# Cross attention of a streaming encoder on Trainium2: keys turned by VectorE's block transpose instead of TensorE

## The chip, the cores and the metric

The kernel runs on one core of a Trainium2 chip (trn2). A core has TensorE (matrix multiplications, with a separate path that loads the stationary operand), VectorE, ScalarE, GpSimd, and SyncE, which here only issues DMA transfers. In the profile they are PE (PEld for the weight loads), DVE, ACT, POOL and SP. The metric is the device time of one execution in microseconds; lower is better.

## What is computed

The reference is one inference step of a two-layer encoder. Each layer has a mixer, a cross attention to a memory, and a SwiGLU block. The change touches the cross attention, which runs twice (once per layer):

```python
def cross_attn(h, mk, mv, w_q, w_o):
    b, t, _ = h.shape
    q = (h @ w_q).reshape(b, t, X_HEADS, X_HEAD_DIM)
    s = jnp.einsum('bqhd,bkhd->bhqk', q, mk).astype(jnp.float32) * X_SCALE
    p = jax.nn.softmax(s, axis=-1).astype(mv.dtype)
    o = jnp.einsum('bhqk,bkhd->bqhd', p, mv).reshape(b, t, X_WIDTH)
    return o @ w_o
```

There are 4 heads of 256 dimensions and 256 memory tokens. One prompt stream of 512 rows attends to keys and values that the kernel computed itself earlier in the step (`memory_kv`; the kernel keeps them in DRAM as `kvd`). Eight running streams of 16 rows each attend to their own cached keys and values, `cache_mem_k` and `cache_mem_v`, of shape (2, 8, 256, 4, 256). All is float32.

## The kernel before

The 640 rows (512 prompt, 128 sample) stay in SBUF in `X`. Products of activations and weights are made in three passes: both operands are split into a rounded high part and the rest (`split_unit`, lines 142 to 153, for weights; `evac_split`, lines 220 to 226, for activations), and high x high, high x low, low x high are added up in PSUM (`PASSES`, `gemm`, lines 191 to 208). A weight unit holds 1024 floats per partition; there are two buffers for the raw unit, three each for the high and low parts.

Scores need the queries and the keys with the head's dimensions on the partitions. The memory's keys lie with the tokens on the partitions after a plain load, so they have to be turned.

`cross_phase` (line 811) is run for layer 0 and layer 1. Its pieces, each a list of small steps:

- `q_list(h)` (line 822) loads the q weights of head h as two units, one per 128 columns (`dt`), each over all eight k-blocks of 128 rows, and makes q with the weights as the stationary operand: 2 halves of 320 columns x 2 `dt` x 24 matmuls (8 k-blocks, 3 passes). Before, its list has 14 steps.
- `load_key(n)` (line 917) asks for the n-th cached key block (one stream, one head, 256 tokens x 256 dimensions, 256 KB) with one DMA into one of four `kr` buffers. `AHEAD = 3`: the step that uses block n asks for block n+3.
- `sample_list(pr, bq)` (line 925) treats two heads and four streams: eight `keys` steps, four loads of values, then `scores`, `trans`, `values`, `turn`. Its `keys` step (line 929) turns a block with four TensorE transposes of 128x128 into a PSUM bank (line 938) and copies it to `KT`, every other one by VectorE (line 942) and by ScalarE (line 944).
- `prompt_list(h)` (line 859) treats one head of the prompt: `load` (two DMAs, line 866), `keys` (four transposes, line 873, then the split of keys and values), and twice `scores`, `trans`, `values`.
- `out_list(h)` (line 999) multiplies the head's output by `w_o` and adds it to `X` (`add_x`, line 316).

`merge` (line 210) deals the steps of several lists into one order by their relative place in their list. After the q of heads 0 and 1, four merges follow, and then the rest of the output projection:

```python
merge(sample_list(0, 0), prompt_list(0), q_list(2))
merge(sample_list(0, 1), prompt_list(1), q_list(3))
merge(sample_list(1, 0), prompt_list(2), out_steps(0))
merge(sample_list(1, 1), prompt_list(3), out_steps(1))
```

This order is a priority: the framework plans the order of each engine's instructions from it and may let a later instruction that is ready pass one that waits. Each engine then works its own instructions strictly in that planned order, and SyncE issues all DMA transfers in one queue. A buffer's next use waits for the last reader of its former content.

The same block transpose on VectorE is already used for the cached keys of layer 0's mixer (line 678), whose blocks are asked for in four DMAs of 32 partitions each (line 670), and for the cached latents of layer 1's mixer (line 1550, loads at line 1545).

Of the kernel before, what the change touches and what calls it, by code (L numbers as in the profile page):

```python
# [18 lines left out]
P = 128  # L19
D = 1024  # L20
KD = D // P
# [71 lines left out]
def fox_mla_kernel(ctx: ExitStack, tc: tile.TileContext, I, O):  # L93
# [717 lines left out]
    def cross_phase(l, nx, rest):  # L811
        w_q, w_o = I["w_x_q"][l], I["w_x_o"][l]
        mk = I["cache_mem_k"][l].rearrange("b (m p) h d -> p (b m) (h d)", p=P)
        mv = I["cache_mem_v"][l].rearrange("b (m p) h d -> p (b m) (h d)", p=P)
        with tc.tile_pool(name=f"x{l}", bufs=2, reuse_waits="tile") as xp:
# [6 lines left out]
            def q_list(h):  # L822
# [4 lines left out]
                def load(dt):  # L827
                    if dt == 0:
                        qs_[h] = [xp.tile([P, 2, NP], F32R, tag=f"qT{i}", name=f"qT{i}", bufs=2) for i in range(2)]
                    c0 = h * XD + dt * P  # L830
                    d[dt] = load_w([(0, P, w_q[:, c0:c0 + P])], per=8)
# [11 lines left out]
                for half in range(2):  # L843
                    for dt in range(2):
                        if half == 0:
                            L.append(lambda dt=dt: load(dt))
                        L += gemm(lambda dt=dt, half=half: ws_ops(d[dt], slice(0, P), nx.T,
                                                                  slice(half * HALF, (half + 1) * HALF), KD),
                                  HALF, lambda ps, dt=dt, half=half: done(ps, dt, half), parts=3)
                return L  # L850
# [8 lines left out]
            def prompt_list(h):  # L859
                d = {}  # L860

                def load():
                    kv = npool.tile([P, 2, 2, XD], F32, tag="gb", name="kv", bufs=1)
                    d["kv"] = [kv[:, i] for i in range(2)]
                    for i in range(2):
                        S.dma_start(kv[:, i], kvd[l][i].rearrange("(t p) n -> p t n", p=P)[:, :, h * XD:(h + 1) * XD])

                def keys():
                    d["kT"] = [xp.tile([P, 2, NMEM], F32R, tag=f"kT{i}", name=f"kT{i}", bufs=1) for i in range(2)]
                    pt = psum_t()  # L870
                    for dt in range(2):
                        for mt in range(2):
                            T.transpose(out=pt[:, dt * NMEM + mt * P:dt * NMEM + (mt + 1) * P],
                                        in_=d["kv"][0][:, mt, dt * P:(dt + 1) * P], identity=ident)
                    evac_split(d["kT"][0], d["kT"][1], pt.rearrange("p (d m) -> p d m", m=NMEM))
                    d["v"] = [xp.tile([P, 2, XD], F32R, tag=f"v{i}", name=f"v{i}", bufs=1) for i in range(2)]
                    evac_split(d["v"][0], d["v"][1], d["kv"][1])
# [137 lines left out]
            for f in ql[:6] + rest[:1] + ql[6:8] + rest[1:] + ql[8:] + q_list(1):  # L1015
                f()
# [760 lines left out]
```

## Time and profile before

| | |
|---|---|
| Median of three runs | 2092.91 us (2092.85 to 2095.61) |
| The profiled execution | 2094.26 us, of which its span is 2092.4 us |
| TensorE busy | 2035.6 us (97%) |
| VectorE busy | 1390.7 us (66%) |
| ScalarE busy | 888.0 us (42%) |
| Granted TensorE clock, mean | 0.996 |
| Cross attention, layer 0: q from about 530 us, four merges | 560.7 to 687.6 us |
| Cross attention, layer 1: four merges | 1480 to 1607 us |

The page gives the busy time of each engine over the span, and then the span in 40 equal slices of 52 us, with the busy share in tenths. A share of the whole span says little of one stage; the views by stretch, by line and in order of time do, and their rows stand in the section after the next. A matmul's duration in the list is the time from its start to its last result and overlaps with the next one's, so the cost of a matmul in a stream is the distance from start to start.

### The profile page before, as it was taken

What the parts mean: (1) busy time and instruction counts of PE and PEld (TensorE: products, weight loads), DVE (VectorE), ACT (ScalarE), POOL (GpSimd) and SP (SyncE); (2) the same over time, 40 slices, a digit from 0 to 9 for tenths busy, and PEclk for the clock granted to TensorE, in tenths of its full rate; (3) what the DMA queues carried; (4) which work ended last, traced back from release to release, by engine and by line L of the source; (5) the groups of instructions that cost most, each with busy time, mean ns of one, the idle gap of its engine ahead of it and who ended that gap; (6) DMA issues with size and microseconds to landing.
All of it is one profiled execution on the core that took longest, in us unless ns stands there. A gap on an engine that the chain in (4) does not pass through costs nothing. (4 is left out here: it accounts for less than half of the span.)

```text
span 2092.4 us, 34811 instructions
## 1 busy us (share of the span) xinstructions
PE 2035.6 (97%) x13629; PEld 1818.6 (87%) x13629; DVE 1390.7 (66%) x2657; ACT 888.0 (42%) x1723; POOL 196.0 (9%) x398
## 2 busy tenths in 40 slices
PE   8999999999999999999999989999999999999998
PEld 7888888877987899999998978887987899999997
DVE  5455555655556896686687567767556896686686
ACT  4343444454443453343344455554443443343342
POOL 1222222220100000000001311100000000000000
PEclk9999999999999999999999999999999999999999
DMA  7565655467554322232221342113454322232221
GB/s 195 114 150 122 164 130 144 147 227 234 164 182 137 103 88 73 80 102 71 81 81 47 104 118 53 53 51 101 146 191 134 104 81 73 80 101 71 81 81 61
DMA packets 334059, 236.37 MB, mean 113 GB/s; under 512 B 99124, under 2 KB 298420, under 8 KB 333896
## 3 DMA queue, kind: packets, MB, share of 16 engines
q1 hardware_dynamic: 333896, 234.15, 38.7%
q8 instruction: 108, 1.77, 0.4%
q14 instruction: 55, 0.45, 0.1%
HBM read 216.90 MB, written 17.21 MB: 112 GB/s over the span
## 5 line engine op out<-in xcount | busy, mean ns | idle before, releaser
L204 PE MATMUL mm<-hT,whi 128*128 128x320 f32 x1744 | 288.9, 312 | 2.9 <-ACT hT L222 2.9
L151 DVE TENSOR_TENSOR wlo<-raw,whi 128x1024 fp32r<-128x1024 f32 (+4 forms) x145 | 169.7, 1173 | 162.8 <-ACT whi L150 124.2
L204 PEld LDWEIGHTS mm<-hT,whi 128*128 128x128 f32 x1744 | 261.9, 189 | 6.8 <-ACT hT L222 4.3
L318 DVE TENSOR_TENSOR X<-mm,X 128x512 f32<-128x512 f32 x270 | 183.5, 686 | 121.7 <-PE mm L204 120.0
L150 ACT CAST whi<-raw 128x1024 fp32r<-128x1024 f32 (+4 forms) x145 | 144.9, 1003 | 151.2 <-PE mm L204 74.7
L204 PE MATMUL mm<-whi,oT 128*128 128x512 f32 x544 | 181.3, 410 | 2.6 <-ACT oT L1679 1.3
L1118 ACT CAST whi<-tw 128x512 fp32r<-128x512 f32 (+1 forms) x120 | 91.9, 766 | 213.8 <-PE mm L204 127.5
L204 PE MATMUL mm<-whi,aT 128*128 128x512 f32 x560 | 173.0, 390 | 1.1 <-ACT aT L1083 1.1
L204 PE MATMUL mm<-hT,wlo 128*128 128x320 f32 x872 | 156.7, 312 | 0.0
L204 PEld LDWEIGHTS mm<-hT,wlo 128*128 128x128 f32 x872 | 133.3, 188 | 3.3 <-issue 3.2
L232 POOL TENSOR_SCALAR rstd<-ss 128x1 f32<-128x1 f32 x49 | 16.4, 334 | 1266.5 <-ACT hn L230 1262.1
L204 PE MATMUL mm<-s,whi 128*128 128x320 f32 x768 | 128.2, 309 | 0.0
L204 PE MATMUL mm<-whi,hT 128*128 128x256 f32 (+2 forms) x800 | 126.3, 296 | 1.3 <-ACT hT L222 0.9
L204 PEld LDWEIGHTS mm<-whi,aT 128*128 128x128 f32 x560 | 104.4, 188 | 23.3 <-ACT aT L1083 1.9
L204 PEld LDWEIGHTS mm<-whi,oT 128*128 128x128 f32 x544 | 97.5, 190 | 25.1 <-DVE X L318 3.8
L204 PEld LDWEIGHTS mm<-s,whi 128*128 128x128 f32 x768 | 116.6, 188 | 0.0
L1119 DVE TENSOR_TENSOR wlo<-tw,whi 128x512 fp32r<-128x512 f32 (+1 forms) x120 | 103.4, 862 | 18.8 <-ACT whi L1118 17.7
L204 PEld LDWEIGHTS mm<-whi,hT 128*128 128x128 f32 x800 | 109.5, 192 | 5.4 <-issue 1.7
L204 PE MATMUL mm<-wlo,oT 128*128 128x512 f32 x272 | 109.5, 403 | 0.0
L204 PE MATMUL mm<-wlo,aT 128*128 128x512 f32 x280 | 108.8, 389 | 0.0
L1118 ACT CAST whi<-raw 128x1024 fp32r<-128x1024 f32 x44 | 46.3, 1052 | 131.7 <-PE mm L204 70.6
L204 PE MATMUL ps_s<-whi,aT 128*128 128x512 f32 x320 | 98.6, 389 | 0.0
(334 smaller groups left out, 4194.1 us busy)
## 6 DMA issues: line engine op xcount, KB each, us to landing
rawg<-w_ffn_gu SPq DMA_DIRECT2D x80, 512.0 KB, 3.8
raw<-w_ffn_down SPq DMA_DIRECT2D x44, 512.0 KB, 3.6
raw<-w_x_kv SPq DMA_DIRECT2D x32, 512.0 KB, 4.4
kr<-cache_mem_k SPq DMA_DIRECT2D x64, 256.0 KB, 3.5
vr<-cache_mem_v SPq DMA_DIRECT2D x32, 512.0 KB, 6.4
raw<-w_fox_in SPq DMA_DIRECT2D x30, 512.0 KB, 4.3
kr<-cache_fox_k SPq DMA_DIRECT2D x64, 128.0 KB, 5.0
vr<-cache_fox_v SPq DMA_DIRECT2D x16, 512.0 KB, 5.6
```

The lines of the kernel that those rows point to most:

```text
L150: A.copy(hi[:, 0:m], raw[:, 0:m])
L151: V.tensor_tensor(lo[:, 0:m], raw[:, 0:m], hi[:, 0:m].bitcast(F32), ALU.subtract)
L204: T.matmul(st["ps"][:, 0:n], lhsT=l, rhs=r, start=(j == 0), stop=(j == m - 1))
L232: G.tensor_scalar(r, ss, EPS, None, ALU.add)
L318: V.tensor_tensor(xs, ps, xs, ALU.add)
L1118: A.copy(hi[:, o:o + m], src)
L1119: V.tensor_tensor(lo[:, o:o + m], src, hi[:, o:o + m].bitcast(F32), ALU.subtract)
```

## The change

A 32x32 block transpose turns each block of 32 partitions by 32 elements in place, so partition group 32g of the result holds what lay on partition group 32g. The cached keys are therefore loaded in another layout: the tokens of a block of 32 on 32 partitions, and the head's 256 dimensions as four runs of 64, one for each group of 32 partitions. `fill_keys` does this with four DMAs of 32 partitions x 8 token blocks x 64 floats, instead of one DMA with 1 KB pieces. `turn_keys` then turns a key block in one VectorE instruction that reads every second float (`t` is the parity of the dimension), and writes `KT` directly; the TensorE transposes and the copies from PSUM are gone. Partition n of the result holds dimensions 2n and 2n+1, so the q weights are taken with the same step of two columns as the stationary operand. For this a head's q weights are loaded together: two units of four k-blocks x 256 columns in place of two units of eight k-blocks x 128 columns.

The prompt's keys, read from `kvd`, take the same way: four DMAs, one block transpose into a tile `kt` (in the buffer of `osb`), and the split from there. The order of steps changes by one step: `q_list` has one load at its start (13 steps), where it had two.

```diff
-        mk = I["cache_mem_k"][l].rearrange("b (m p) h d -> p (b m) (h d)", p=P)
+        mk = I["cache_mem_k"][l].rearrange("b (m j) h d -> b j m (h d)", j=32)
...
-                def load(dt):
-                    if dt == 0:
-                        qs_[h] = [xp.tile([P, 2, NP], F32R, tag=f"qT{i}", name=f"qT{i}", bufs=2) for i in range(2)]
-                    c0 = h * XD + dt * P
-                    d[dt] = load_w([(0, P, w_q[:, c0:c0 + P])], per=8)
+                def load():
+                    qs_[h] = [xp.tile([P, 2, NP], F32R, tag=f"qT{i}", name=f"qT{i}", bufs=2) for i in range(2)]
+                    d["w"] = load_w([(0, XD, w_q[:, h * XD:(h + 1) * XD])])
+
+                def ops(dt, half):
+
+                    hs = slice(half * HALF, (half + 1) * HALF)
+                    return [(d["w"].get(wi, k).rearrange("p (n t) -> p t n", t=2)[:, dt], nx.T[ai][:, k, hs])
+                            for wi, ai in PASSES for k in range(KD)]
...
                 for half in range(2):
                     for dt in range(2):
-                        if half == 0:
-                            L.append(lambda dt=dt: load(dt))
-                        L += gemm(lambda dt=dt, half=half: ws_ops(d[dt], slice(0, P), nx.T,
-                                                                  slice(half * HALF, (half + 1) * HALF), KD),
-                                  HALF, lambda ps, dt=dt, half=half: done(ps, dt, half), parts=3)
-                return L
+                        L += gemm(lambda dt=dt, half=half: ops(dt, half), HALF,
+                                  lambda ps, dt=dt, half=half: done(ps, dt, half), parts=3)
+                return [load] + L
+
+            def fill_keys(r, src, h):
+
+                for g in range(4):
+                    c0 = h * XD + 64 * g
+                    S.dma_start(r[32 * g:32 * g + 32], src[:, :, c0:c0 + 64])
+
+            def turn_keys(dst, r):
+                V.transpose(dst, r.rearrange("p m (i t) -> p t m i", t=2))
...
                 def load():
-                    kv = npool.tile([P, 2, 2, XD], F32, tag="gb", name="kv", bufs=1)
-                    d["kv"] = [kv[:, i] for i in range(2)]
-                    for i in range(2):
-                        S.dma_start(kv[:, i], kvd[l][i].rearrange("(t p) n -> p t n", p=P)[:, :, h * XD:(h + 1) * XD])
+                    kv = npool.tile([P, 2, 512], F32, tag="gb", name="kv", bufs=1)
+                    d["k"] = kv[:, 0].rearrange("p (m i) -> p m i", m=8)
+                    fill_keys(d["k"], kvd[l][0].rearrange("(m j) n -> j m n", j=32), h)
+                    d["vr"] = kv[:, 1].rearrange("p (t n) -> p t n", t=2)
+                    S.dma_start(d["vr"], kvd[l][1].rearrange("(t p) n -> p t n", p=P)[:, :, h * XD:(h + 1) * XD])
 
                 def keys():
                     d["kT"] = [xp.tile([P, 2, NMEM], F32R, tag=f"kT{i}", name=f"kT{i}", bufs=1) for i in range(2)]
-                    pt = psum_t()
-                    for dt in range(2):
-                        for mt in range(2):
-                            T.transpose(out=pt[:, dt * NMEM + mt * P:dt * NMEM + (mt + 1) * P],
-                                        in_=d["kv"][0][:, mt, dt * P:(dt + 1) * P], identity=ident)
-                    evac_split(d["kT"][0], d["kT"][1], pt.rearrange("p (d m) -> p d m", m=NMEM))
+                    kt = xp.tile([P, 2, NMEM], F32, tag="osb", name="kt", bufs=1)
+                    turn_keys(kt, d["k"])
+                    evac_split(d["kT"][0], d["kT"][1], kt)
                     d["v"] = [xp.tile([P, 2, XD], F32R, tag=f"v{i}", name=f"v{i}", bufs=1) for i in range(2)]
-                    evac_split(d["v"][0], d["v"][1], d["kv"][1])
+                    evac_split(d["v"][0], d["v"][1], d["vr"])
...
-                    hc = slice((2 * pr + hh) * XD, (2 * pr + hh + 1) * XD)
-                    krs[n] = xp.tile([P, 2, XD], F32, tag="kr", name="kr", bufs=4)
-                    S.dma_start(krs[n], mk[:, 2 * (4 * bq + b):2 * (4 * bq + b) + 2, hc])
+                    krs[n] = xp.tile([P, 8, 64], F32, tag="kr", name="kr", bufs=4)
+                    fill_keys(krs[n], mk[4 * bq + b], 2 * pr + hh)
...
-                    kr = krs.pop(n)
                     if b % 2 == 0:
                         d["KT"][hh, b // 2] = xp.tile([P, 2, 2, NMEM], F32, tag="KT", name="KT", bufs=4)
-                    pt = psum_t()
-                    for dt in range(2):
-                        for mt in range(2):
-                            T.transpose(out=pt[:, dt * NMEM + mt * P:dt * NMEM + (mt + 1) * P],
-                                        in_=kr[:, mt, dt * P:(dt + 1) * P], identity=ident)
-                    src = pt.rearrange("p (d m) -> p d m", m=NMEM)
-                    if b % 2 == 0:
-                        V.tensor_copy(d["KT"][hh, b // 2][:, 0], src)
-                    else:
-                        A.copy(d["KT"][hh, b // 2][:, 1], src)
+                    turn_keys(d["KT"][hh, b // 2][:, b % 2], krs.pop(n))
...
-            for f in ql[:6] + rest[:1] + ql[6:8] + rest[1:] + ql[8:] + q_list(1):
+            for f in ql[:5] + rest[:1] + ql[5:7] + rest[1:] + ql[7:] + q_list(1):
```

## Rows read from the trace of the kernel before

**Rows 1.** The page: busy time by engine, and the span in 40 slices.

```profile
span 2092.4 us, 34811 instructions
PE 2035.6 (97%) x13629; PEld 1818.6 (87%) x13629; DVE 1390.7 (66%) x2657; ACT 888.0 (42%) x1723; POOL 196.0 (9%) x398
...
PEclk9999999999999999999999999999999999999999
DMA  7565655467554322232221342113454322232221
```

**Rows 2.** Busy time by stretch: the four merges of layer 0's cross attention.

```profile
core 0: us, PE busy (x) PEld busy (x) DVE busy (x) ACT busy (x) POOL busy (x), PEclk, DMA share, GB/s
560.70:590.20 29.50, 29.40 (x257) 26.60 (x256) 13.30 (x29) 12.43 (x30) 0.00 (x0) 1.00 0.54 164
590.20:620.80 30.60, 30.17 (x260) 26.86 (x259) 14.89 (x33) 13.35 (x33) 0.00 (x0) 1.00 0.58 189
620.80:654.00 33.20, 32.27 (x239) 25.54 (x237) 22.14 (x43) 12.93 (x30) 0.00 (x0) 1.00 0.53 173
654.00:687.60 33.60, 33.53 (x238) 26.39 (x237) 22.23 (x44) 12.02 (x28) 0.00 (x0) 1.00 0.41 138
```

**Rows 3.** The same view: all four merges of layer 0 and of layer 1.

```profile
560.70:687.60 126.90, 125.38 (x986) 105.39 (x985) 72.56 (x148) 50.73 (x118) 0.00 (x0) 1.00 0.51 165
1480.40:1607.00 126.60, 126.00 (x972) 110.77 (x972) 67.15 (x135) 51.06 (x115) 0.00 (x0) 1.00 0.52 168
```

**Rows 4.** Groups by line and shape: busy us, mean ns | idle before, releaser.

```profile
L938 PE MATMUL ps_t<-cst,kr 128*128 128x128 f32 x256 | 37.5, 274 | 1.6 <-DMA kr<-cache_mem_k 1.6
L873 PE MATMUL ps_t<-cst,kv 128*128 128x128 f32 x32 | 5.1, 283 | 0.0
L942 DVE COPY KT<-ps_t 128x512 f32<-128x512 f32 x32 | 22.0, 687 | 7.9 <-PE ps_t L938 7.9
L678 DVE STREAM_TRANSPOSE KT<-kr 128x512 f32<-128x512 f32 x32 | 21.5, 691 | 0.0
L944 ACT COPY KT<-ps_t 128x512 f32<-128x512 f32 x32 | 18.8, 587 | 19.7 <-PE ps_t L938 19.3
```

**Rows 5.** In order of time, first merge: start us, us, engine, line, operation, count.

```profile
569.88 0.80 PE L897 MATMUL ps_t<-cst,hn 128*128 128x128 f32 x4
...
571.69 0.60 PE L938 MATMUL ps_t<-cst,kr 128*128 128x128 f32 x4
...
572.04 1.41 PE L204 MATMUL mm<-hT,wlo 128*128 128x320 f32 x8
...
573.29 0.40 PE L218 MATMUL ps_o<-PT,v 128*128 128x256 f32 x2
```

**Rows 6.** In order of time, q matmuls ahead of the merges.

```profile
545.46 1.34 PE L204 MATMUL mm<-hT,wlo 128*128 128x320 f32 x8
545.70 1.05 ACT L150 CAST whi<-raw 128x1024 fp32r<-128x1024 f32 x1 [0.47 <-PE mm L204]
...
546.63 2.51 PE L204 MATMUL mm<-hT,whi 128*128 128x320 f32 x16
```

**Rows 7.** In order of time, first merge: key groups, scores, and a passed wait.

```profile
562.75 0.60 PE L938 MATMUL ps_t<-cst,kr 128*128 128x128 f32 x4
...
564.80 0.60 PE L938 MATMUL ps_t<-cst,kr 128*128 128x128 f32 x4
...
566.41 0.60 PE L938 MATMUL ps_t<-cst,kr 128*128 128x128 f32 x4
566.76 1.67 PE L218 MATMUL ps_s<-kT,qT 128*128 128x256 f32 x12
...
568.27 1.34 PE L204 MATMUL mm<-hT,whi 128*128 128x320 f32 x8
...
582.49 2.15 PE L204 MATMUL mm<-hT,whi 128*128 128x320 f32 x13
...
584.74 0.41 PE L960 MATMUL ps_t<-cst,pws 128*128 128x128 f32 x2
```

**Rows 8.** Groups of TensorE in layer 0's four merges: busy, mean | idle.

```profile
L204 PE MATMUL mm<-whi,oT 128*128 128x512 f32 x80 | 26.5, 406 | 0.0
L204 PE MATMUL mm<-hT,whi 128*128 128x320 f32 x128 | 22.1, 316 | 0.0
L938 PE MATMUL ps_t<-cst,kr 128*128 128x128 f32 x128 | 18.8, 274 | 1.3 <-DMA kr<-cache_mem_k 1.3
```

**Rows 9.** DMA issues: KB each, us to landing; and issue times, ns min/median/max.

```profile
kr<-cache_fox_k SPq DMA_DIRECT2D x64, 128.0 KB, 5.0
...
cb<-cache_mla_ckv SPq DMA_DIRECT2D x64, 32.0 KB, 2.4
...
L923 SPq DMA_DIRECT2D kr<-cache_mem_k x64: 367/368/687, 518.1 to 1598.4; - x64
...
L1545 SPq DMA_DIRECT2D cb<-cache_mla_ckv x64: 311/449/1282, 1133.0 to 1301.7; - x64
```

**Rows 10.** Busy time by stretch: a feed-forward window, and the first mixer's attention.

```profile
746.00:774.00 28.00, 28.00 (x193) 28.00 (x192) 26.54 (x49) 13.56 (x24) 0.00 (x0) 1.00 0.29 86
...
110.00:300.00 190.00, 187.57 (x1487) 160.72 (x1487) 112.05 (x296) 79.51 (x179) 48.18 (x96) 1.00 0.60 140
```

**Rows 11.** Weight loads of TensorE by line: busy us, mean ns | idle.

```profile
L204 PEld LDWEIGHTS mm<-hT,whi 128*128 128x128 f32 x1744 | 261.9, 189 | 6.8 <-ACT hT L222 4.3 <-DVE KT L678 1.3 <-issue 0.4
...
L974 PEld LDWEIGHTS ps_o<-vr,PTs 128*32 128x32 f32 x256 | 7.5, 109 | 6.4 <-ACT PTs L962 2.2
...
L1606 PEld LDWEIGHTS ps_o<-H,H 128*64 128x64 f32 x64 | 3.5, 137 | 0.7 <-issue 0.4 <-PE ps_s L218 0.4
```

## The prediction

> **What bounds the kernel now.** I read the page's busy times first [rows 1]. TensorE is busy 97% of the span and the granted clock is full in every slice (2.4 GHz, the upper of its two levels), so a step that leaves TensorE should be worth its own time there, as long as its wait does not stay behind. The reader is to see the other engines too: VectorE 66%, ScalarE 42%, DMA between one and seven tenths of a slice. Next I cut the first cross attention into its four merges [rows 2]: TensorE is idle 0.10, 0.43, 0.93 and 0.07 us in them. VectorE is at 45%, 49%, 67% and 66%, and the DMA engines at 0.41 to 0.58. The second cross attention is alike: 126.6 us for its four merges beside 126.9 [rows 3]. So each merge is TensorE's, with VectorE second in the last two. The page's chain of waits covers only the last microseconds and says nothing here.
>
> **The 288 transposes that leave TensorE.** Each cached key block (64 of them) and each prompt head (8) is turned by four transposes: 256 and 32 instructions [rows 4]. Their listed durations overlap, so I price a group by starts. From 571.69 to 573.29, 1.60 us, TensorE does one group and eight q matmuls [rows 5]; undisturbed, eight such matmuls take 545.46 to 546.63, 1.17 us [rows 6]. A group costs 0.43 us, 72 groups 31.0 us. All of it lies on TensorE's path. TensorE's idle time before the cached groups, 1.6 us, for late keys [rows 4], I count as neither gained nor lost: the wait moves to VectorE with the key.
>
> **What VectorE takes over.** 72 block transposes. The same size stands in the trace, 128x512 f32 from SBUF, 691 ns [rows 4]: 49.8 us. Away go 32 copies of 687 ns, 22.0 us, so VectorE gains 27.7 us, 3.5 us per merge; ScalarE loses 32 copies of 587 ns, 18.8 us. The prompt's split into two parts stays, now read from SBUF. Nine groups less make a merge 3.9 us shorter, so VectorE goes to (13.30+3.5)/25.6 = 66% in the first kind and (22.14+3.5)/29.3 = 88% in the second [rows 2]. That is cover, but thin. The lower bound of what VectorE then costs TensorE is nothing; the upper, with VectorE the bound there and also standing 1 us for each of four closely spaced keys, is 25.6+4 = 29.6 us against 29.3, plus a lost overlap about as large as the softmax chain between scores and transposes, from 568.27 to 569.88, 1.6 us [rows 5, 7]: about 2 us in each of four merges, 8 us. I take the idle that the third merge shows today, 0.93 us, in each of the four wide merges: 3.7 us. It is nearest, being a wait for a late key in a wide merge [rows 2, 8].
>
> The new transpose reads every second float, which no VectorE row shows. From below it cannot beat 691 ns by much, since 512 elements are still written; from above I let it double. I take 691 ns. Doubled, the wide merges need 25.6+6.2 = 31.8 us of VectorE against 29.3, 10 us in four merges, and the gain falls to some 17 us.
>
> **A new wait, and who stands behind it.** Before, a late key stopped TensorE; now it stops VectorE, with the splits, the residual adds and the softmax's reduce, reciprocal and scaling queued behind, and behind those TensorE's PSUM buffers and transposes. The turned keys themselves are wanted only by the sample scores, after all eight. The lead is three turns as before: 562.75, 564.80 and 566.41 are the starts of consecutive groups [rows 7], 1.8 us apart, so some 5 us, and about 4.2 us once the groups are gone. A key needs four issues, 0.37 to 0.45 us each, and a landing of 2.4 us (same count of pieces, 32 partitions) to 5.0 us (the attention stage's keys, 128 KB an issue) [rows 9]: 3.5 to 6.8 us. So VectorE will stand about 0 to 2.6 us for keys in the dense half of a merge. In the narrow merges it has 9 us spare; the wide ones are the 3.7 us above.
>
> **SyncE and the DMA engines.** SyncE issues 192 more for the cached keys and 24 more for the prompt's; w_q keeps its 16. In a merge that is 27 more, 10 to 12 us of its queue. Queued there are values, w_q, w_o and the prompt's keys; each is asked for a merge or several microseconds ahead, and in these merges TensorE's matmul groups of line 204 stand idle for no weight or value load [rows 8]. I take nothing, and up to 0.4 us a merge as upper bound, 3 us. Packets: a merge's key blocks go from 2304 of 1 KB to 9216 of 256 B. The merges, mostly 1 KB pieces, show 0.51x16/165 = 49 ns per KB; the feed-forward window, 512 B weight rows alone, 0.29x16/86 = 54 ns per KB, 27 ns a piece [rows 3, 10]. A 256 B piece lies between a quarter of 49 and 27 ns, estimated at 16 (on the line through both). Keys then take 9.2 us of the engines per merge (15.6 at the upper end) instead of 7.1; the engines, at 64.7 us of 126.9 now, reach 73 to 99 of 111. Not the bound, so nothing.
>
> The Trainium skill (DMA: Bandwidth & Descriptors, Specifications) speaks against this edit: it wants 512 B at least for line rate, because below that the engine reads, modifies and writes. In the trace the attention stage, with its 128 B key pieces, shows 0.60x16/140 = 69 ns per KB over a mix [rows 10], dearer than the merges but far from a collapse. What the rule would do at its worst is the fifth case below.
>
> **The q weights.** Their loads become two units of four k-blocks by 256 columns, so a gemm needs both units. The cast of the second waits for the slot that the previous head releases at the twelfth of its last 24 matmuls; then twelve matmuls and the next head's first four pass, 16 x 0.147 = 2.35 us [rows 6], over a cast of 1.05 us. Hidden; uncovered it would be 1.05 us in each of eight heads, 8 us. I take none.
>
> TensorE now loads its stationary block with a step of two floats: 2 phases x 4 heads x 2 x 2 gemms of 24 = 768 loads. No row shows such a load. Loads of 32, 64 and 128 columns take 109, 137 and 189 ns [rows 11], so 0.83 ns a column, 107 ns, and 256-column matmuls run every 126 ns (566.76 to 568.27, twelve) [rows 7], so a load fits in 126. The q matmuls go every 147 ns [rows 6]: 21 to 40 ns are free. A step of two walks 1024 bytes of a partition in that time, 7 B/ns, while the moving side walks 1280 bytes in 147 ns, 8.7 B/ns, already. So I take no cost; the upper bound is a doubled load, 214 ns, 67 ns x 768 = 51 us.
>
> **Sum.** 31.0 removed, 3.7 given back: 27.3 us. The profiled execution took 2094.26 us (span 2092.4), 0.06% over the median of the runs, 2092.91. The difference carries over: 2092.9 - 27.3 = 2066 us.
>
> **The cases.** (1) Forecast: most of the 31 us arrives, 2056 to 2074 us. For it: TensorE idle under 1 us in a merge; the trace's order shows that waiting instructions are passed by ready ones (the two transposes of 584.74 sit between q matmuls [rows 7]). Lower end: the 1.6 us of idle and another 4 us of waits go too. (2) VectorE stands for keys or runs its transposes slowly, and TensorE pays in the wide merges: the 8, 3 and 8 us of bounds above, or the doubled transpose: 2075 to 2088. For it 88%; against it, that the keys' results are not urgent. (3) Nothing: TensorE waits where it transposed, since softmax chains of 1.6 us set the pace and the groups only filled them; 2089 to 2097. For it the groups between scores and transposes; against it the fill, which TensorE always had. (4) Slower, in the gemms of q: the step-two load takes twice the time and TensorE's pace becomes 214 ns; it decides from 147 ns on. 2066 + 51 = 2117, and as soon as a load takes over 183 ns the 27 us are gone. For it that no row has the form; against it the 8.7 B/ns. (5) Slower by DMA: a 256 B piece costs as much as 1 KB, 50 ns: 28.8 us for keys plus 9.1 us of the rest is 38 us a merge against 31.7, and 8 x 6.2 = 50 us: some 2143. Against it: pieces of 512 B at 27 ns.
>
> **Chances.** (1) 0.60, (2) 0.20, (3) 0.06, (4) 0.09, (5) 0.05. The range takes in (1) and (2), whose ends come from the bounds: 2054 to 2088. A measurement can tell some 0.2%, 4.2 us, from no change: faster (1) and (2), 0.80; same (3), 0.06; slower (4) and (5), 0.14.
>
> **What the changed profile would show.** No transposes of keys on TensorE and 72 transposes on VectorE near 0.69 us; merges of about 26 and 30 us; q matmuls still every 147 ns and loads of 189 ns (else case 4); VectorE idle for keys by DMA of a few microseconds in all, and its wide merges under 90% (else case 2); DMA share in the merges of 0.65 to 0.85 (else case 5). The forecast is wrong if the merges shorten by less than 3 us each, or if idle time of TensorE in them rises over 1.5 us.

## The result, and the profile after

The changed kernel takes 2148.59 us (median of four, 2146.55 to 2149.18), the kernel before 2093.85 beside it: ratio 1.0256, 95% interval 1.0244 to 1.0268. It is 54.7 us slower; 2066 us and a range to 2088 had been predicted. The profiled execution has a span of 2146.7 us.

The page after (answering to [rows 1]; PEclk is the granted clock in tenths of 2.4 GHz):

```profile
span 2146.7 us, 34530 instructions
...
PE 2040.8 (95%) x13341; PEld 1803.8 (84%) x13341; DVE 1417.5 (66%) x2697; ACT 868.9 (40%) x1691; POOL 196.9 (9%) x398
...
PEclk9999999999989999999999999999999999999999
```

288 matmul instructions are gone, as planned, and yet TensorE is 5 us longer busy, and idle 105.9 us of the span in place of 56.8. The stretches of layer 0's four merges show where (as [rows 2]: us, busy us of PE, PEld, DVE, ACT, POOL, granted clock, DMA share, GB/s):

```profile
566.00:601.00 35.00, 29.17 (x219) 24.41 (x218) 17.14 (x37) 10.71 (x27) 0.00 (x0) 0.90 0.60 138
601.00:640.00 39.00, 31.16 (x219) 23.88 (x218) 18.74 (x39) 11.38 (x28) 0.00 (x0) 0.94 0.61 150
640.00:680.00 40.00, 31.84 (x191) 22.52 (x190) 23.63 (x45) 9.38 (x22) 0.00 (x0) 0.93 0.62 150
680.00:716.00 36.00, 31.62 (x203) 23.11 (x202) 22.86 (x44) 10.34 (x23) 0.00 (x0) 1.00 0.41 139
```

They take 150 us, where they took 126.9 [rows 3]. TensorE is idle 5.8, 7.8, 8.2 and 4.4 us in them, and its clock is full only in the last. No other engine is near its limit: VectorE has 48% to 64%, and the DMA share is 0.41 to 0.62.

What TensorE does at the end of the first merge, in order of time (start us, us; in brackets the idle time before, and who ended it):

```profile
583.22 1.33 PE L204 MATMUL mm<-hT,wlo 128*128 128x320 f32 x8
584.49 0.62 PE L948 MATMUL ps_s<-KT,Qp 128*32 128x256 f32 x2
585.99 1.05 PE L948 MATMUL ps_s<-KT,Qp 128*32 128x256 f32 x10 [0.88 <-DVE KT L860]
588.83 0.41 PE L957 MATMUL ps_t<-cst,pws 128*128 128x128 f32 x2 [1.79 <-DVE pws L331]
589.70 2.77 PE L971 MATMUL ps_o<-vr,PTs 128*32 128x256 f32 x32 [0.46 <-ACT PTs L959]
593.18 2.93 PE L218 MATMUL ps_o<-PT,v 128*128 128x256 f32 x12 [0.71 <-ACT osb L976]
595.91 1.06 PE L981 MATMUL ps_t<-cst,osb 128*128 128x128 f32 x4
598.95 2.98 PE L204 MATMUL mm<-hT,whi 128*128 128x320 f32 x17 [1.99 <-ACT whi L150]
```

From 584.49 on there is no projection matmul for 14 us. The sample's tail (its scores, transposes, values and the `turn` of its output) follows with only the prompt's values (L218) in it: each step waits for VectorE or ScalarE to finish with the step before, and the next merge then waits for its weights. Such a tail is called bare below, and projection matmuls that stand between its steps are called fill. Before, q matmuls lay there ([rows 7]: the 13 ahead of the transposes at 584.74). The idle time also costs the clock (busy time by stretch):

```profile
586.00:588.00 2.00, 1.04 (x10) 0.36 (x10) 0.42 (x1) 0.47 (x2) 0.00 (x0) 1.00 0.74 181
588.00:590.00 2.00, 0.71 (x10) 0.41 (x14) 1.83 (x5) 0.47 (x3) 0.00 (x0) 1.00 1.05 273
590.00:592.00 2.00, 2.00 (x32) 0.91 (x24) 0.49 (x1) 0.00 (x0) 0.00 (x0) 0.67 0.74 196
592.00:594.00 2.00, 1.29 (x12) 0.82 (x5) 0.00 (x0) 0.59 (x1) 0.00 (x0) 0.50 1.09 343
594.00:596.00 2.00, 2.00 (x11) 2.00 (x11) 0.00 (x0) 0.00 (x0) 0.00 (x0) 0.50 1.33 187
```

TensorE is busy 1.04 and 0.71 us in the first two rows; then the clock falls, and from 592 us it is at 0.50, the lower level of 1.2 GHz. Why the work stands so late is in SyncE's queue (issues in order of time; the second number is the time of the whole group):

```profile
555.29 7.89 SPq L857 DMA_DIRECT2D kr<-cache_mem_k  x16
563.22 0.45 SPq L964 DMA_DIRECT2D vr<-cache_mem_v  x1
570.93 2.81 SPq L857 DMA_DIRECT2D kr<-cache_mem_k  x4
573.84 0.40 SPq L964 DMA_DIRECT2D vr<-cache_mem_v  x1
...
586.64 1.93 SPq L857 DMA_DIRECT2D kr<-cache_mem_k  x4
588.67 1.19 SPq L148 DMA_DIRECT2D raw<-w_x_q  x2
```

16 issues, four key blocks, go out by 563.2; then the ring of four `kr` buffers is full, and SyncE stands until the turn of a key block frees one. The values and, at 588.67, the next merge's weights are queued behind keys. The last four of this merge's eight key turns have their data, but come late in VectorE's own order: they start at 570.20, 578.16, 583.52 and 585.23. In all, VectorE was idle only 1.2 us for keys (line, shape, count, busy us, mean ns, idle before and its cause; and the page's issues: KB, us to landing):

```profile
L860 DVE STREAM_TRANSPOSE KT<-kr 128x512 f32<-128x512 f32 x64 | 43.1, 694 | 1.2 <-DMA kr<-cache_mem_k 1.2
...
kr<-cache_mem_k SPq DMA_DIRECT2D x256, 64.0 KB, 3.0
```

TensorE's longest waits in layer 0's merges (us in total, times, longest; all of them come to 26.0):

```profile
PE ps_t L957 <- DVE pws L331: 7.2, 4, 1.8
PE mm L204 <- ACT whi L150: 6.8, 3, 2.4
PE ps_s L948 <- DVE KT L860: 5.1, 4, 1.4
PE ps_o L218 <- ACT osb L976: 2.8, 4, 0.7
```

The score matmuls themselves take longer as well, since the late key turns break the 16 of a merge into two or three groups. By line, first in the kernel before, then in the changed one (both layers):

```profile
L951 PE MATMUL ps_s<-KT,Qp 128*32 128x256 f32 x256 | 15.5, 382 | 0.0
L948 PE MATMUL ps_s<-KT,Qp 128*32 128x256 f32 x256 | 28.8, 386 | 10.8 <-DVE KT L860 10.8
```

### The profile page after: what moved, and what is told of

Its sections match the earlier page's. It is cut to its first block, busy times and chain, and to the rows that moved or that the text cites. A ratio compares the mean times of both kernels' runs of the same rounds, so it can differ in the third digit from the quotient of the medians.

```text
span 2146.7 us, 34530 instructions
## 1 busy us (share of the span) xinstructions
PE 2040.8 (95%) x13341; PEld 1803.8 (84%) x13341; DVE 1417.5 (66%) x2697; ACT 868.9 (40%) x1691; POOL 196.9 (9%) x398
```

## The theories

**First:** the turn on VectorE is cheap and worth about 30 us. The loss comes from four issues per key block: with them the planned order is another one, in which turns, values and next weights come late and the sample's tail stands bare. **Second:** VectorE's turn, in its in-order queue, is the cause however the keys come. **Third:** the joined q weights are late. **Fourth:** the issues, or the 256-byte pieces, cost by themselves.

All runs, each with its ratio to the kernel before on the same chip:

| kernel | median us | ratio, 95% interval |
|---|---|---|
| before, q weights joined | 2091.9 | 0.9994 [0.9982, 1.0005] |
| before, four issues per key block | 2098.9 | 1.0021 [1.0007, 1.0035] |
| changed, one issue of 1 KB pieces | 2052.7 | 0.9804 [0.9776, 0.9833] |
| changed, one issue of 256 B pieces | 2056.3 | 0.982 [0.9792, 0.9849] |
| changed, four issues of 1 KB pieces | 2107.1 | 1.0061 [1.0038, 1.0084] |
| one issue, tail made bare | 2099.2 | 1.0031 [1.0017, 1.0045] |
| changed, fill held behind the tail | 2140.7 | 1.0226 [1.0189, 1.0262] |
| changed, keys issued by GpSimd | 2135.2 | 1.0198 [1.0173, 1.0224] |
| two heads per issue (512 B) | 2110.7 | 1.0083 [1.0053, 1.0112] |
| same, keys issued by GpSimd | 2081.4 | 0.9945 [0.9928, 0.9961] |
| two heads, prompt turned by TensorE | 2084.1 | 0.9958 [0.9947, 0.997] |
| same, keys issued by GpSimd | 2079.4 | 0.9925 [0.9902, 0.9948] |
| same, weights and values by GpSimd instead | 2081.7 | 0.9931 [0.9896, 0.9966] |
| that, ring of 3 / of 4 key blocks | 2107.8 / 2114.1 | 1.0065 [1.0043, 1.0088] / 1.0096 [1.0067, 1.0125] |
| that with ring of 2, GpSimd from the second merge on | 2062.0 | 0.9846 [0.983, 0.9861] |
| same, query copies shared with VectorE | 2058.0 | 0.9823 [0.9806, 0.9841] |

The kernels with one issue per key block, and the changed one with four issues of 1 KB pieces, do all the work in its shapes, but their samples attend to permuted keys: they are experiments and cannot replace the changed kernel.

The planned order of TensorE's instructions at the end of layer 0's second merge, as the kernels hold it (S sample scores, T its transposes, W its values, U its turn; q, o projection; p, t prompt; the number counts instructions, and the profile lists each S and W twice):

```
before                    S16 t4 q13 T2 q4 W16 q5 p12 q2 U4
before, four issues       S16 t4 q13 T2 q4 W10 q7 W6 p12 U4
one issue, 1 KB           S16 q8 t4 q7 T2 q6 W16 q3 o2 p12 U4
one issue, 256 B          S16 q8 t4 q7 T2 q6 W16 q3 o2 p12 U4
four issues, 1 KB         S1 p1 S9 q1 p11 q7 S1 t4 q16 S5 T2 W16 p12 U4
changed                   S9 q8 t4 q8 S1 q8 S6 T2 W16 p12 U4
one issue, tail made bare S16 T2 W16 U4
two heads, 512 B          S3 q8 t1 q3 t3 q13 S13 T2 W16 p12 U4
two heads, keys by GpSimd S16 q8 t4 q4 T2 q9 W16 q3 o2 p12 U4
two heads, prompt on PE   S16 q8 t4 q1 T2 q7 W8 q8 W8 p12 U4
the last kernel           S16 q8 t4 q6 T2 q7 W16 q3 o2 p12 U4
```

## The parts one by one

**The q weights alone.** The kernel before with the joined load of the diff, columns taken without a step:

```diff
-                    d[dt] = load_w([(0, P, w_q[:, c0:c0 + P])], per=8)
+                    d["w"] = load_w([(0, XD, w_q[:, h * XD:(h + 1) * XD])])
...
+                    return [(d["w"].get(wi, k)[:, dt * P:(dt + 1) * P], nx.T[ai][:, k, hs])
+                            for wi, ai in PASSES for k in range(KD)]
```

> The kernel before with one edit: the query weights of a head come in two units, as in the changed kernel. First theory: no change, 2088 to 2099 us. Second: no change. Third theory (two units make the weights late): 2110 us or more.

2091.9 us: no change. The third theory falls.

**Four issues alone.** The kernel before with

```diff
-                    S.dma_start(krs[n], mk[:, 2 * (4 * bq + b):2 * (4 * bq + b) + 2, hc])
+                    for g in range(4):
+                        ps = slice(32 * g, 32 * g + 32)
+                        S.dma_start(krs[n][ps], mk[ps, 2 * (4 * bq + b):2 * (4 * bq + b) + 2, hc])
```

> The kernel before with one edit: a block of cached keys is fetched by four DMAs of 32 partitions, in 1 KB pieces. First theory: the fill between the sample's steps stays in the written-out order, so 2088 to 2102 us. A theory that four issues cost time by themselves on SyncE's queue (192 more issues): 2110 us or more.

2098.9 us, 5.4 more than before beside it: 192 issues cost little where the order stays nearly as it was. In the second merge the 16 scores still stand together with fill behind them, and only the values are cut in two.

**One issue.** The changed kernel with `fill_keys` of the cached blocks replaced by

```diff
+            def fill_big(r, n):
...
+                for g in range(1):
+                    ps = slice(0, P)
+                    S.dma_start(r[ps].rearrange("p (t x) i -> p t (x i)", t=2), mkb[ps, 2 * (4 * bq + b):2 * (4 * bq + b) + 2, hc])
...
-                    fill_keys(krs[n], mk[4 * bq + b], 2 * pr + hh)
+                    fill_big(krs[n], n)
```

where `mkb` is the view of the kernel before.

> The changed kernel with the cached keys of a block fetched by one DMA of 1 KB pieces, as the kernel before fetches them, and still turned by VectorE. The keys then stand in another order than the values, so the sample attention is of permuted keys; all the work and its shapes stay. First theory (the turn is cheap and worth about 30 us; what costs is that a block's keys are asked for by four issues of 256-byte pieces, which puts the last turns, the values and the next weights late in the written-out order, so that the sample tail runs with nothing beside it): about 2066 us, 2058 to 2078, the four merges of layer 0 at 27 to 30 us each, TensorE idle under 1.5 us in each and its granted clock at 0.99 to 1.00 there. Second theory (VectorE with the turn is the bound, however the keys come): 2130 us or more. Third theory (the query weights in two units per head make the weights late): 2110 us or more.

2052.7 us, below the range expected. The second theory falls: with the same 72 turns on VectorE the kernel is 40.8 us faster than before. All eight key turns of a merge now run ahead of it: those of the first merge end by 550.5 us, and those of the second run from 574.80 to 582.5, beside the first one's tail. From the first merge's `turn` step to the fourth's, TensorE is never idle in layer 0, and VectorE reaches 83% (stretches from `turn` step to `turn` step):

```profile
583.70:609.50 25.80, 25.80 (x225) 23.36 (x224) 17.76 (x39) 11.19 (x28) 0.00 (x0) 1.00 0.77 225
609.50:637.00 27.50, 27.50 (x197) 21.49 (x196) 22.84 (x46) 9.49 (x22) 0.00 (x0) 1.00 0.75 218
637.00:661.80 24.80, 24.80 (x185) 19.00 (x182) 17.53 (x37) 9.38 (x22) 0.00 (x0) 1.00 0.40 140
```

Its tail of the first merge has fill between all steps, and no wait:

```profile
573.66 1.93 PE L956 MATMUL ps_s<-KT,Qp 128*32 128x256 f32 x32
575.53 1.45 PE L204 MATMUL mm<-hT,whi 128*128 128x320 f32 x8
...
578.29 0.38 PE L965 MATMUL ps_t<-cst,pws 128*128 128x128 f32 x2
578.42 0.40 PE L204 MATMUL mm<-hT,whi 128*128 128x320 f32 x1
...
579.48 1.93 PE L979 MATMUL ps_o<-vr,PTs 128*32 128x256 f32 x32
581.35 0.71 PE L204 MATMUL mm<-hT,wlo 128*128 128x320 f32 x3
```

**Four issues of 1 KB pieces** in that kernel:

```diff
+                for g in range(4):
+                    ps = slice(32 * g, 32 * g + 32)
+                    S.dma_start(r[ps].rearrange("p (t x) i -> p t (x i)", t=2), mkb[ps, 2 * (4 * bq + b):2 * (4 * bq + b) + 2, hc])
```

> As the run before it, but the keys of a block are fetched by four DMAs of 32 partitions each with two pieces of 1 KB per partition; again the keys stand in another order than the values. It has the four issues of the changed kernel without its 256-byte pieces. First theory: between the one-issue kernel and the changed one, 2080 to 2130 us; near 2066 would leave the piece size as the cause, near 2148 the number of issues alone. Second theory: 2130 us or more. Third: 2110 or more.

2107.1 us: 54.4 us for the step from one issue to four. On the kernel before the same step cost 5.4, and there the order changed little. Here it leaves the tail bare in the second to the fourth merge, and the score matmuls, broken into groups, are listed with 26.7 us in place of 15.5.

**One issue of 256-byte pieces** in that kernel:

```diff
+                c0 = (2 * pr + hh) * XD + 64 * b
+                S.dma_start(r, mkb[:, 8 * bq:8 * bq + 8, c0:c0 + 64])
```

> The changed kernel with each key block fetched by one DMA, as in the one-issue kernel, but in pieces of 256 bytes in place of 1 KB: one block then holds 64 dimensions of four streams, so the sample attention is of permuted keys, while all bytes, instructions and shapes stay, and the written-out order is nearly that of the one-issue kernel. First theory (the pieces cost little by themselves, the order that four issues bring costs): 2050 to 2062 us. Rival (pieces of 256 bytes cost on the DMA rings, whatever the order): 2075 us or more.

2056.3 us: 49,152 more packets cost 3.6 us. So the small pieces are not the cause by themselves, and with the 5.4 us for the issues alone the fourth theory falls too.

**The order alone.** The one-issue kernel with nothing changed but order: `tc.issue_after` queues the sample scores behind the merge's last projection matmul, and the next merge's projection behind the `turn` step; the tail also stands last in the merge's list of steps.

```diff
+                                with tc.issue_after(behind["fill"].ins):
                                     T.matmul(sp[32 * b:32 * b + 32, 0:NMEM], lhsT=Q[:, 2 * hh + dt, 4 * bq + b, :],
...
+                        with tc.issue_after(behind["turn"].ins):
+                            f()
```

> The kernel with one DMA of 1 KB pieces per key block (keys in another order than the values, as in that run, 2052.7 us), with one more edit, in the written-out order alone: the sample's scores, transposes, values and turn of a merge are held behind the merge's projection matmuls, and the next merge's projection behind them, in three of the four merges of each layer. No DMA, weight or VectorE instruction changes. First theory (a sample tail without fill costs by itself: its waits for VectorE and ScalarE and TensorE's clock after them): 3 to 7 us for each of the six bare tails, so 2070 to 2095 us, with the granted clock under 0.97 in the merges. Rival (the order is harmless; the changed kernel lost its time to the DMA transfers themselves): 2050 to 2058 us.

2099.2 us: 46.5 us for six bare tails, 7.8 each, a little over the range. The first of them:

```profile
580.86 1.93 PE L959 MATMUL ps_s<-KT,Qp 128*32 128x256 f32 x32
585.62 0.69 PE L968 MATMUL ps_t<-cst,pws 128*128 128x128 f32 x2 [2.82 <-DVE pws L333]
586.76 3.64 PE L982 MATMUL ps_o<-vr,PTs 128*32 128x256 f32 x32 [0.46 <-ACT PTs L970]
591.14 1.12 PE L992 MATMUL ps_t<-cst,osb 128*128 128x128 f32 x4 [0.73 <-ACT osb L987]
591.91 4.04 PE L204 MATMUL mm<-hT,whi 128*128 128x320 f32 x16
```

The price can be read here: 4.0 us of waits (2.82+0.46+0.73), and at the lower clock the values take 3.64 in place of 1.93 us and 16 q matmuls 4.04 in place of 2.51 [rows 6], 3.2 us more. That is 7.2 of 7.8. The two profiled executions say the same of all six: TensorE is 26.2 us longer idle and 20.2 us longer busy. The mechanism seen in the changed kernel is thus shown to cost this much with the best of key loads.

**The order alone, put back.** The changed kernel, with the projection steps that follow the sample's tail in program order queued behind its last instruction so far:

```diff
+            if n == 2 and "pe" in behind:
+                with tc.issue_after(behind["pe"].ins):
+                    lists[n][i]()
```

> The changed kernel with one edit, in the written-out order alone: the projection matmuls that follow the sample's scores, transposes and values in program order are held behind them on TensorE, so that they lie between those steps again. First theory: the waits inside the tail and the low clock go, the late keys and the late weights of the next merge stay: 2105 to 2135 us. Rival (the transfers themselves cost the time): 2143 to 2155 us.

2140.7 us, only 7.9 less, and a miss: I expected 2105 to 2135, and the rival named 2143 to 2155. The median lies between the two; what speaks against the rival is the one issue of 256-byte pieces, not this run. TensorE's waits moved (us in total, times, longest; layer 0):

```profile
PE ps_s L956 <- DVE KT L868: 8.3, 4, 2.1
PE mm L204 <- ACT whi L150: 5.9, 3, 2.1
PE ps_o L979 <- DMA vr<-cache_mem_v: 5.4, 2, 4.1
```

In the changed kernel the waits for turned keys had been 5.1 and for values 1.8. When fill stands inside the tail, less of it stands ahead, and the late turns and values are met sooner. In the third and fourth merge, moreover, no fill came between the scores and their transposes. So the bare tail is what TensorE shows, but below it lies the lateness of keys, values and weights in SyncE's and VectorE's orders.

**Keys off SyncE's queue.** The changed kernel with

```diff
-                    S.dma_start(r[32 * g:32 * g + 32], src[:, :, c0:c0 + 64])
+                    eng.dma_start(r[32 * g:32 * g + 32], src[:, :, c0:c0 + 64])
```

where `eng` is GpSimd for the cached keys:

> The changed kernel with one edit: the cached keys' four DMAs per block, with their 256-byte pieces, are issued by GpSimd in place of SyncE. The transfers are the same; SyncE's queue then holds only weights, values and the prompt's keys and no longer stands behind a key buffer. In the written-out order the weights come early, but the last score matmuls of a merge stand far behind, after up to 60 projection matmuls, and in the later merges the tail is bare. First theory (late weights and values behind the key issues are a part of the loss, the bare tails another): 2100 to 2135 us, with no wait of TensorE for a weight cast at the start of a merge. Rival (the transfers of 256-byte pieces themselves): 2140 us or more.

2135.2 us, 13.4 less: just above the first theory's range and below the rival's. No wait for weights is left in layer 0's merges; the scores wait 7.9 us for turned keys (5.1 in the changed kernel). The run is no clean price of late weights, since more changed than the queue's owner: the planned order is another one, and the transfers are not the same, for the profile lists GpSimd's keys as 8192 packets where SyncE's queue now has 69,632 fewer. Late weights are a part; most of the loss stays without them.

## Towards a kernel that keeps the gain

One issue cannot fetch a block in the turned layout: each group of 32 partitions holds other dimensions of the same tokens. But two heads lie side by side in memory. With 128 dimensions per partition group, groups 0 and 1 of one head, 2 and 3 of the next, four issues fetch twice as much, in 512-byte pieces. The sample queries are put on matching partitions, with zeros for the other head; the 16 score matmuls stay 16.

```diff
+                    for g in range(4):
+                        c0 = 2 * pr * XD + 128 * g
+                        S.dma_start(krs[n][32 * g:32 * g + 32], mk[4 * bq + b][:, :, c0:c0 + 128])
...
+                        for g in range(2):
+                            for s in range(2):
+                                A.activation(Q[z + 32 * g:z + 32 * g + 32, 2 * s + dt, :, o:o + TS],
+                                             ps[64 * g + 32 * s:64 * g + 32 * s + 32, n:HALF].rearrange("p (b t) -> p b t", t=TS),
+                                             AF.Copy, scale=X_SCALE)
```

> The changed kernel with the cached keys of two heads fetched together: four issues for a block of 256 tokens and two heads, in pieces of 512 bytes, so 64 issues per layer in place of 128, and two turns of 128x512 for each block; the queries of the samples are put on the partitions to match by four ScalarE copies in place of one. The prompt's keys as in the changed kernel. The first merge of a layer has fill around the sample tail again, the three others not. First theory (the order and the small pieces cost): 2085 to 2125 us. Rival (pieces under 1 KB cost whatever the order): 2125 to 2150 us.

> As the run before it, but the prompt's keys are fetched by one DMA and turned by TensorE, as in the kernel before; so only 64 + 4 key issues per layer are left, and the sample tail has fill around it in all merges. First theory: the one-issue kernel's 2052.7 us, plus eight groups of transposes at 0.43 us (3.4 us), so 2056 us, 2050 to 2068. Rival (pieces of 512 bytes in four issues cost by themselves): 2080 us or more. Second theory (VectorE's turn is the cause): 2120 or more.

2110.7 and 2084.1 us. The order went as the counts of issues let one expect, and each step with fewer issues is faster. The second was expected at 2056, though: in layer 0's merges TensorE waited twice for weights, 4.8 us in all, and the clock fell to 0.83 from 640 to 660 us.

With the keys issued by GpSimd:

> The kernel with keys of two heads fetched together in 512-byte pieces (2110.7 us), with one more edit: the cached keys are issued by GpSimd in place of SyncE. In the written-out order all merges have fill around the sample tail and weights and values are asked for a merge ahead. First theory: the loss goes wholly, 2048 to 2064 us, near the one-issue kernel's 2052.7. Rival (pieces of 512 bytes or GpSimd's issues cost by themselves): 2075 us or more.

> The kernel with keys of two heads fetched together and the prompt's keys turned by TensorE (2084.1 us), with one more edit: the cached keys are issued by GpSimd in place of SyncE, which takes the two waits of TensorE for late weights out of its merges. First theory: 2050 to 2066 us, some 3 us above the kernel that turns the prompt's keys on VectorE. Rival: 2075 us or more.

2081.4 and 2079.4 us: the first gained 29 us, the second 5, and neither reached its expected range. In the first, the same number of issues now comes from another queue, and the planned order has its fill again. With keys on SyncE and the merges' weights and values on GpSimd instead, and with longer rings of keys:

> The kernel with keys of two heads fetched together and the prompt's keys turned by TensorE (2084.1 us), with one more edit: in the four merges the weights and the values are asked for by GpSimd, so that SyncE's queue holds the keys and nothing stands behind a key that waits for its buffer. If what was left in the kernel whose keys GpSimd issues (2079.4 us) came from its 128 issues: 2055 to 2066 us. If the ring of two key blocks, too short a lead, is the remainder: 2072 to 2085 us.

> As the run before it, with three key blocks in the ring (asked for two ahead) and three tiles of turned keys in place of two and four: the scores of the first stream of a merge then come ahead of the others. If the short ring is the remainder: 2053 to 2064 us, and 10 us or more below the run before it. If not: within 4 us of it.

> As the run before it, with four key blocks in the ring (asked for three ahead) and two tiles of turned keys: the scores of two streams come ahead of the others. If the short ring is the remainder: 2053 to 2062 us. If the score bank that is held longer delays the prompt's scores: slower than with three blocks, 2062 us or more.

2081.7, 2107.8 and 2114.1 us. The first fitted the short ring in number, but the two others do not bear that out, and they were no clean test: to free the buffers, their scores are made stream by stream, and these cost TensorE 46.0 us in place of 15.5 (by line; ring of three, then ring of two):

```profile
L958 PE MATMUL ps_s<-KT,Qp 128*32 128x256 f32 x256 | 46.0, 383 | 0.0
```

```profile
L958 PE MATMUL ps_s<-KT,Qp 128*32 128x256 f32 x256 | 15.5, 382 | 0.0
```

30.5 us more busy time is over the 26.1 that the ring of three lost, so a longer ring may have been worth some 4 us (5 with the ring of four: 53.3 us, 37.8 more, for 32.4 lost); nothing more can be taken from it. The profile of the ring of two says where its loss lies in layer 0: ahead of 580 us, in the first merge, where weights from GpSimd came late. At 568 us ScalarE had waited 4.6 us for them, and the prompt's key split behind it kept TensorE waiting 3.6 us. So in the next run SyncE keeps the first merge's weights and values, and GpSimd asks from the second merge on; in the last, VectorE makes two of the four query copies.

```diff
+            wdma[0] = G
             merge(sample_list(0, 1), prompt_list(1), q_list(3))
```

> The kernel with keys of two heads fetched together and the prompt's keys turned by TensorE (2084.1 us), with one more edit: from the second merge of a layer on, weights and values are asked for by GpSimd; in the first merge by SyncE as before. In that kernel the first merge was undisturbed and the second and third waited for weights; with all on GpSimd it was the other way round. If late weights are the remainder: 2056 to 2066 us. If not: 2074 us or more.

> As the run before it, with two of the four small copies of the samples' queries done by VectorE in place of ScalarE, so that the PSUM bank is free some 0.5 us earlier. If the copies hold TensorE up: 3 to 8 us below the run before it. If not: within 2 us of it.

2062.0 and 2058.0 us, both as the first condition said. The last kernel is 1.8% faster than before and 90.6 us faster than the changed one. Its merges, from `turn` step to `turn` step, stand as full as the one-issue kernel's:

```profile
585.00:611.20 26.20, 26.20 (x227) 23.71 (x226) 18.57 (x41) 11.67 (x31) 4.11 (x6) 1.00 0.74 217
611.20:639.40 28.20, 28.11 (x201) 21.88 (x200) 22.96 (x46) 10.02 (x24) 4.63 (x7) 1.00 0.83 213
639.40:664.60 25.20, 25.20 (x187) 19.41 (x186) 19.43 (x39) 9.45 (x22) 3.36 (x5) 1.00 0.55 163
```

## Why the prediction was wrong

- **What bounds the kernel, and the 288 transposes.** Right. Mis-sized by a fifth: in the one-issue kernel TensorE's busy time fell from 2035.6 to 1998.0 us, 0.52 us a group if all of it is theirs, where the starts had given 0.43. Idle time fell by 4.4 us as well.
- **What VectorE takes over.** The turn costs 694 ns with its step of two, as forecast 691; doubled it never was. VectorE came to 83% in the one-issue kernel's wide merge, where 88% was forecast, and the 3.7 us to be given back did not show.
- **"A new wait, and who stands behind it"** failed in its reasoning. It asked whether the data would be there in time; it was (1.2 us of idle in all). The lower end of its sum, 3.5 us, counts three of the four issues (4 x 0.37 + 2.4 is 3.9), and nothing hangs on that. What was late was the key turn's place in VectorE's order. "The turned keys themselves are wanted only by the sample scores" was taken as a comfort; but a turn also frees the buffer that SyncE's whole queue waits for.
- **"SyncE and the DMA engines" is the step that failed.** It counted the 27 more issues of a merge as 10 to 12 us of queue time beside idle queue, on the ground that what is queued there "is asked for a merge or several microseconds ahead". That lead belonged to the old order. After the change, values and weights were issued behind keys that wait for a buffer; it took nothing for this and gave 3 us as the bound. From one issue to four is 54.4 us. The sum held each engine's order fixed, while the section on the kernel before says that the framework plans it.
- **The DMA's price.** One issue of 256-byte pieces lets the queue's packets take 41.2% of 2054.6 us where 1 KB pieces took 39.5% of 2050.4, times 16 engines 585 us for 49,152 packets more. With 49 ns for each of the 16,384 large ones, a small piece took 21 ns, between the 16 taken and the bound of 27. The time moved by 3.6 us; the fifth case, +50 us by dear pieces, is excluded. The Trainium skill (DMA: Bandwidth & Descriptors, Specifications) puts line rate at 512 B and more; a piece that costs 21 ns for a quarter of the bytes fits that direction, and the runs show that it did not matter here.
- **The q weights.** Right: the joined load costs nothing (0.9994), and at full clock ahead of the merges, TensorE's loads with the step of two take 196 ns in the mean, 188 before, and the q matmuls still come every 147 ns, as forecast. The fourth case is excluded.
- **The rivals.** "Nothing: TensorE waits where it transposed" came nearest in mechanism: TensorE waits in the softmax chains, but what it lacks there is the projection's fill, not the transposes. It ended at 2148 and not at 2097, since the idle time also brought the lower clock and the weights of the next merge came late. No slower case named the order.
- **What would make it wrong** was named rightly: idle time over 1.5 us in a merge. It was 4.4 to 8.2.

Open: between the one-issue kernel and the changed one lie 96 us. The two profiled executions divide them as TensorE sees them: 53.5 us more idle and 42.8 us more busy. Of the busy time the score matmuls are 13.3 us (28.8 listed in place of 15.5), and the granted clock, 0.987 in the mean where it was 0.998, would make some 24 us of 2147, an estimate. By cause the division is less complete. Six bare tails cost 46.5 us by experiment, and the changed kernel has eight. How the rest divides among late keys, values and weights isn't settled, since they overlap: restoring the fill gave 7.9, freeing the weights 13.4. From four issues of 1 KB to four of 256 B is 41.5 us, while the same pieces in one issue cost 3.6; that the order (bare in the first merge too) makes this difference is argued from the orders, not isolated. The landings support it: 64 KB took 3.0 us with the small pieces and 2.5 with the large ones (medians). Nor does any trace show why the planner orders as it does; shown is only that the order changed with the number of issues per block, and with the queue that makes them.

## What to carry to other kernels

When instructions are ordered by a planner, a change of a transfer's shape can reorder every engine: compare the planned order around the serial chains (scores, softmax, values) before adding up costs. Count a transfer by its issues and by who is queued behind them for a ring buffer, not by its bytes alone. Where a layout needs several issues, make each fetch more (two heads here), and keep weights and values out of the queue that waits for the ring.

## What the runs showed of the hardware

- A bare tail cost 7.8 us in the mean of six. In the first of them 4.0 us were waits; after them TensorE was granted 0.50 of its clock (1.2 GHz) from 586 to 594 us, and the 32 listed values matmuls took 3.64 us for 1.93.
- The 256 listed score matmuls, of 32 columns at four column positions, took 15.5 us when the positions alternate. They took 46.0 and 53.3 us in the two kernels that score stream by stream, where four instructions in a row go to one position (and one part of PSUM). One took 382 or 383 ns in each.
- A DMA of 32 partitions x 8 pieces of 256 bytes took SyncE 448 ns to issue (median) and GpSimd 582 ns.
- A weight load of 128 columns took 196 ns when read with a step of two floats and 188 ns without; 320-column matmuls came every 147 ns with either.
- The 32x32 block transpose of 128x512 floats took 686 to 694 ns, read with a step of one or of two floats.
